# A hybrid mLSTM and gated-delta encoder block: modulation rows in a tile of their own, asked for three quanta ahead of pinned sums

## The chip, the cores and the metric

The kernel runs on one core of a Trainium2 chip. The core's engines run side by side, each through its own list of instructions in order: TensorE (PE; its weight loads are PEld), VectorE (DVE), ScalarE (ACT), GpSimd (POOL) and SyncE (SP). Here SP does nothing but ask for transfers (DMA) from the chip's memory into the core's on-chip memory. An instruction that waits for a semaphore holds up all that stands behind it on its engine. The metric is the device time of one execution in microseconds (us); lower is better.

## The reference, cut to what matters

One encoder block on a sequence of 256 tokens with 2048 channels, everything in float32:

```python
mod = silu(c) @ ada_w + ada_b                      # (1, 6 * 2048)
shift_m, scale_m, gate_m, shift_f, scale_f, gate_f = jnp.split(mod, 6, axis=-1)
h = rms_norm(x, norm_mix_w) * (1 + scale_m) + shift_m
(a_q, a_k, a_v, a_o, a_i, a_f, b_qkv, b_z, b_beta, b_a, merge) = split(h @ w_in)
y_a = (sigmoid(a_o) * rms_norm(mlstm(...))) @ w_branch_a      # 4 heads, both directions
y_b = (rms_norm(gated_delta(...)) * silu(b_z)) @ w_branch_b   # 16 heads, both directions
g_a, g_b = split(sigmoid(merge))
x = x + gate_m * ((g_a * y_a + g_b * y_b) @ w_out)
hf = rms_norm(x, norm_ffn_w) * (1 + scale_f) + shift_f
gt, up = split(hf @ w_gate_up)
x = x + gate_f * ((silu(gt) * up) @ w_down)
return rms_norm(x, norm_final_w)
```

The change touches how the last four of the six modulation vectors come to be: gate_m, shift_f, scale_f and gate_f, 2048 numbers each, each a dot product of silu(c) with a column of ada_w.

## The kernel before

**Weights.** Almost all time goes into products of 256 tokens with weight matrices. A weight tile is 1 MB (128 partitions x 2048 numbers, 8 KB in a partition). SP asks for it (line 181 in `fjob`, line 213 in `tjob`) into a ring of three buffers with the tag "raw". Float32 is emulated by a high and a low part: for each half of the tile ACT rounds the high part `wh` (lines 185, 216), DVE subtracts to get the low part `wl` (lines 187, 218), and PE makes three products of each block, `wh` with the high part of the activations, `wh` with their low part, and `wl` with the high part (lines 190 to 192 and 237 to 239). A buffer of the ring is free again once DVE has made `wl` of its second half. A half tile is one step of a job, and the change calls it a quantum. `fjob` puts features on the partitions and makes gated-delta and mLSTM heads (tiles named raw_b, raw_a), `tjob` puts tokens there (raw_z, raw_ma, raw_mb, raw_o, raw_yb, raw_ya, and raw_gt, raw_up, raw_d in the FFN).

**Stages.** The modulation's first two parts are folded into the first product (to about 137 us of the profile). The gates and the first heads follow until 310. Then 16 gated-delta heads go in four groups of four. Each group runs two pairs of heads (`gdn_phase2`, `gdn_blocks`) and then the inversion for the next group (`invert`); the groups' pairs lie at 310 to 440, 495 to 605, 690 to 810 and 870 to 965. These recurrences are chains of small operations on PE, DVE and ACT. Between their steps the code calls `next(pieces)` or `fill()`, which runs one step of a weight job, so that PE has dense work while a chain waits. The mLSTM and the projection `y_b` follow to 1100, then `y_a` and the output projection to 1270, then the FFN: gate and up to 1744, down to 1976.

**The modulation rows.** Parts 2 to 5 are laid out so that a row block is again 128 x 2048 numbers, 1 MB: 16 blocks to a part, 64 in all, named ada2_0 to ada5_15. `add()` (line 114) multiplies a block by silu(c) and sums over the row, one DVE instruction of 2048 columns, whose result is 128 of the part's numbers. `ada_parts` is a generator that hands out these blocks in turn, and `pump()`, called once for every two half tiles, takes a step of it on every `every[0]`-th call. `held` keeps steps back in the first pieces of a pair, and `owed` remembers them. `room` says where the blocks go. In the gated-delta, mLSTM and y_b stages and in the FFN it is the same ring "raw" that the weights stream through, with at most one block asked for at a time; at y_a and the output projection it is a pool of its own, "sr", with three buffers. In the ring's first use a block's sum is added either when the next block is due or when two more weight tiles have been asked for (`raw_tile`).

**What sets the order.** The instructions are written in this order and then moved by a list scheduler; `order(...)` (`keep_in_program_order`) pins an instruction to its place in the program. The sums are pinned only where `room[0][3] > 1`, at y_a and the output projection; elsewhere the scheduler places them. On SP rows and weights stand in one queue.

Of the kernel before, what the change touches and what calls it, by code (L numbers as in the profile page):

```python
# [9 lines left out]
F32 = mybir.dt.float32  # L10
# [5 lines left out]
P = 128  # L16
# [36 lines left out]
def hybrid_block(ctx: ExitStack, tc: tile.TileContext, xr, nfr, crow, pk_d, cst_d, ada2, ada4, win0, winb, wint, wba, wbb, wo, wgu, wd, out, dbg=None):  # L53
# [6 lines left out]
    cp = pool(ctx, "cp")  # L60
    st = pool(ctx, "st")
    acc_ps = pool(ctx, "acc_ps", 4, space=PSUM)
    g_ps = pool(ctx, "g_ps", 4, space=PSUM)
# [42 lines left out]

    room = [(st, "raw", 3, 0)]
    asked, since = [], [0]

    def add():  # L110

        part, b, raw = asked.pop(0)
        c = part * KB + b
        order(V.scalar_tensor_tensor(raw, raw, 1.0, row_c[:, :D], ALU.mult, ALU.mult, accum_out=mod[:, c : c + 1]), room[0][3] > 1)  # L114
        if b == KB - 1:
            c = slice(part * KB, part * KB + KB)
            V.tensor_tensor(mod[:, c], mod[:, c], pk[:, PK_ADAB + c.start : PK_ADAB + c.stop], ALU.add)

    def ada_parts(*parts):

        todo = [(part, b) for part in parts for b in range(KB)]
        while todo or asked:
            pl, tag, bufs, depth = room[0]
            if not depth and asked:
                add()
            while todo and len(asked) < max(depth, 1):
                part, b = todo.pop(0)  # L130
                raw = pl.tile([P, D], F32, tag=tag, bufs=bufs, name=f"ada{part}_{b}")
                nc.sync.dma_start(raw, ada4[part - 2, b])
                asked.append((part, b, raw))
                since[0] = 0
            if depth:
                add()
            yield True

    def raw_tile(shape, name):

        since[0] += 1
        if since[0] > 2 and asked and room[0][0] is st:
            add()
        return st.tile(shape, F32, tag="raw", bufs=3, name=name)
# [10 lines left out]

    background = []
    count, every = [0], [0]
    owed, held = [0], [False]

    def sums(n=1):  # L160

        while n and background:
            if next(background[0], None):
                n -= 1
            else:
                background.pop(0)

    def pump():
        count[0] += 1
        if every[0] and count[0] % every[0] == 0:  # L170
            owed[0] += 1
        if owed[0] and not held[0]:
            owed[0] -= 1
            sums()

    def fjob(name, src, done):

        ps = acc_ps.tile([P, 512], F32, tag="acc", name=f"acc_{name}")
        o = ps[:, :T]
        raw = raw_tile([P, KB, P], f"raw_{name}")  # L180
        nc.sync.dma_start(raw, src)
        for k0 in range(0, KB, 8):
            wh = st.tile([P, 8, P], F32R, tag="wh", bufs=3, name=f"wh_{name}_{k0}")
            wl = st.tile([P, 8, P], F32R, tag="wl", bufs=3, name=f"wl_{name}_{k0}")
            S.activation(wh, raw[:, k0 : k0 + 8], AF.Copy)  # L185
            settle()
            V.tensor_tensor(wl, raw[:, k0 : k0 + 8], wh.bitcast(F32), ALU.subtract)  # L187
            for k in range(8):
                kk = k0 + k
                PE.matmul(o, wh[:, k], woven(hh[:, kk]), start=kk == 0, stop=False)  # L190
                PE.matmul(o, wh[:, k], woven(hl[:, kk]), start=False, stop=False)  # L191
                PE.matmul(o, wl[:, k], woven(hh[:, kk]), start=False, stop=kk == KB - 1)  # L192
            if k0:
                pump()
                done(o.rearrange("p (c h) -> p h c", h=2))
            yield True
# [5 lines left out]
    def tjob(name, chunks, xh, xl, done, early=0, by_token=None, steps=1, parts=((0, slice(0, 512)), (1, slice(0, 512)))):  # L202
# [28 lines left out]
        for n, (u, k0) in enumerate(todo):  # L231
            wh, wl = made.pop(0) if made else halves(u, k0)
            for k in range(2):
                kk = 4 * u + k0 + k
                for t in range(2):
                    c = slice(t * P, (t + 1) * P)
                    order(PE.matmul(ps[t], xh[:, kk, c], woven(wh[:, k]), start=kk == 0, stop=False), early and steps > 1)  # L237
                    PE.matmul(ps[t], xl[:, kk, c], woven(wh[:, k]), start=False, stop=False)  # L238
                    PE.matmul(ps[t], xh[:, kk, c], woven(wl[:, k]), start=False, stop=kk == last)  # L239
            if k0:  # L240
                pump()
                if u == len(chunks) - 1:
                    done(ps)
# [767 lines left out]
    for pair in ((0, 1), (2, 3)):  # L1011
# [5 lines left out]
        for n, _ in enumerate(steps(*(heads1[h] for h in pair))):  # L1017
            fill(3 + n)
    background.append(ada_parts(2, 3, 4))

# [8 lines left out]
    for g in range(4):  # L1029
# [6 lines left out]
        if g == 3:  # L1036
# [4 lines left out]
            for c in first2:  # L1041
                next(c)
        every[0] = (4, 2, 2, 2)[g]
        for p in range(2):
# [17 lines left out]
        if g < 3:  # L1062
            fills.insert(0, z_job(g + 1))
            every[0] = owed[0] = 0
            if asked:
                add()
            invert(g + 1)
# [58 lines left out]
    every[0] = owed[0] = 0  # L1126
    if asked:
        add()
    cores = steps(*first2)
# [23 lines left out]
    drive(cores, 3)  # L1153
    every[0] = 2
    drive(steps(mlstm(2), mlstm(3)), 3)
    every[0] = 1
    fill(1000)
# [29 lines left out]

    every[0] = 2
    for g in range(4):
# [134 lines left out]
    if dbg is not None and "x1" in dbg:  # L1324
        G.dma_start(dbg["x1"], x1)
    room[0] = (st, "raw", 3, 1)
    background.append(ada_parts(5))
    sw.close()
# [71 lines left out]
    next(gt0)  # L1400
    every[0] = 4

# [168 lines left out]
```

## Time and profile before

| | us |
|---|---|
| runs of the kernel: median of 3 | 1991.46 |
| lowest, highest | 1991.42, 1999.04 |
| profiled execution | 1994.34 |
| its span, first to last instruction | 1992.4 |
| TensorE clock granted, mean over the span | 0.991 of full |

The profiled execution is 2.9 us above the median, and 1.9 us of it lie outside its span. The span is what the views divide: busy time of an engine is the time in which one of its instructions runs; a wait is idle time of an engine with the instruction that ended it; the chain of waits goes back from an instruction to what released it. All times in the views count from the start of the span. In the names, wh_a is the high part of a tile raw_a, acc_a the product that uses it, and ada<-ada a block of modulation rows.

### The profile page before, as it was taken

To read this page: it belongs to the slowest core of one execution; us is meant where nothing else is said; L and a number is where in the kernel's file an instruction comes from. 1 tells how busy PE (TensorE), PEld (TensorE's weight loads), DVE (VectorE), ACT (ScalarE), POOL (GpSimd) and SP (SyncE) were. 2 spreads that over 40 slices of the span, in tenths; PEclk is the share of its full clock that TensorE was granted. 3 is DMA by queue.
4 is the path that set the end of the run, shared out by engine and by line. 5 is a ranking of instruction groups with operands and counts; after the bars stand their busy time and mean duration, and the time that the engine had idled before them with its cause. 6 is when DMAs were issued, how large, how long until landed. Compare 5 with 4: busy or idle time off the path is not lost.

```text
span 1992.4 us, 27101 instructions
## 1 busy us (share of the span) xinstructions
PE 1937.3 (97%) x10418; PEld 1708.8 (86%) x10418; DVE 1407.0 (71%) x2067; ACT 1032.8 (52%) x1557; POOL 116.4 (6%) x211
## 2 busy tenths in 40 slices
PE   8999999999999999999999999999999999999998
PEld 6878889998898899889787888888888888888886
DVE  6778887887878798867476878765666665555554
ACT  3137647765666576555444544554444444444444
POOL 0001210111001101010100000200000000000000
PEclk9999999999999999999999999999999999999999
DMA  9987676655667666587786888566676675565653
GB/s 399 420 338 232 190 250 231 222 182 199 232 191 231 222 235 210 197 278 265 255 303 230 351 300 325 176 239 247 235 268 237 234 269 194 200 212 201 210 194 145
DMA packets 78962, 485.64 MB, mean 244 GB/s; under 512 B 10585, under 2 KB 15969, under 8 KB 24433
## 3 DMA queue, kind: packets, MB, share of 16 engines
q1 hardware_dynamic: 63216, 450.69, 62.6%
q0 software_dynamic: 8160, 17.88, 4.0%
q10 hardware_dynamic: 7458, 15.36, 2.0%
q8 instruction: 81, 1.33, 0.3%
q14 instruction: 47, 0.39, 0.1%
HBM read 467.07 MB, written 16.82 MB: 243 GB/s over the span
## 4 chain that ended last, share of the span: by engine, by line
PE 76%; DVE 10%; DMA 8%; ACT 2%; issue 2%; POOL 0%; ACTq 0%; SPq 0%; DVEq 0%; POOLq 0%
PE acc_gt L238 4%; PE acc_gt L237 4%; PE acc_gt L239 4%; PE acc_up L238 4%; PE acc_up L237 4%; PE acc_up L239 4%; PE acc_d L237 4%; PE acc_d L238 4%; PE acc_d L239 4%; DMA ra<-ada 3%; PE acc_o L239 2%; PE acc_o L237 2%; PE acc_o L238 2%; DMA ada<-ada 2%; PE acc_b L190 2%
## 5 line engine op out<-in xcount | busy, mean ns | idle before, releaser
L218 DVE TENSOR_TENSOR wl_d<-raw_d,wh_d 128x1024 fp32r<-128x1024 f32 x88 | 107.7, 1225 | 105.9 <-ACT wh_d L216 105.9
L218 DVE TENSOR_TENSOR wl_up<-raw_up,wh_up 128x1024 fp32r<-128x1024 f32 x88 | 107.7, 1225 | 100.3 <-ACT wh_up L216 100.3
L218 DVE TENSOR_TENSOR wl_gt<-raw_gt,wh_gt 128x1024 fp32r<-128x1024 f32 x88 | 108.2, 1229 | 79.6 <-ACT wh_gt L216 79.5
L190 PE MATMUL acc_b<-hh,wh_b 128*128 128x256 f32 x576 | 163.4, 284 | 0.4 <-ACT wh_b L185 0.4
L192 PE MATMUL acc_b<-hh,wl_b 128*128 128x256 f32 x576 | 160.2, 278 | 1.0 <-DVE wl_b L187 0.9
L191 PE MATMUL acc_b<-hl,wh_b 128*128 128x256 f32 x576 | 159.6, 277 | 0.0
L216 ACT ACTIVATE wh_d<-raw_d 128x1024 fp32r<-128x1024 f32 x88 | 93.0, 1057 | 126.3 <-PE acc_d L238 117.6
L114 DVE SCALAR_TENSOR_TENSOR ada<-ada,crow 128x2048 f32<-128x2048 f32 x64 | 146.4, 2288 | 14.8 <-DMA ada<-ada 14.7
L216 ACT ACTIVATE wh_gt<-raw_gt 128x1024 fp32r<-128x1024 f32 x88 | 92.9, 1056 | 118.6 <-PE acc_gt L238 71.0
L216 ACT ACTIVATE wh_up<-raw_up 128x1024 fp32r<-128x1024 f32 x88 | 92.8, 1055 | 108.1 <-PE acc_up L238 77.1
L237 PE MATMUL acc_gt<-wh_gt,hfh 128*128 128x512 f32 x352 | 135.5, 385 | 0.6 <-ACT hfh L1358 0.6
L238 PE MATMUL acc_gt<-wh_gt,hfl 128*128 128x512 f32 x352 | 135.2, 384 | 0.0
L239 PE MATMUL acc_gt<-wl_gt,hfh 128*128 128x512 f32 x352 | 134.0, 381 | 0.0
L237 PE MATMUL acc_up<-wh_up,hfh 128*128 128x512 f32 x352 | 133.4, 379 | 0.0
L238 PE MATMUL acc_up<-wh_up,hfl 128*128 128x512 f32 x352 | 133.4, 379 | 0.0
L239 PE MATMUL acc_up<-wl_up,hfh 128*128 128x512 f32 x352 | 133.4, 379 | 0.0
L237 PE MATMUL acc_d<-wh_d,ffh 128*128 128x512 f32 x344 | 130.5, 379 | 0.0
L238 PE MATMUL acc_d<-wh_d,ffl 128*128 128x512 f32 x344 | 130.5, 379 | 0.0
L239 PE MATMUL acc_d<-wl_d,ffh 128*128 128x512 f32 x344 | 130.4, 379 | 0.0
L564 PE MATMUL first<-x,raw 128*128 128x256 f32 x512 | 114.5, 382 | 7.6 <-ACT x L558 7.6
L564 PEld LDWEIGHTS first<-x,raw 128*128 128x128 f32 x512 | 96.0, 190 | 26.1 <-ACT x L558 13.6
L192 PEld LDWEIGHTS acc_b<-hh,wl_b 128*128 128x128 f32 x576 | 111.7, 194 | 1.7 <-DVE wl_b L187 1.7
(383 smaller groups left out, 5283.6 us busy)
## 6 DMA issues: line engine op xcount, KB each, us to landing
ada<-ada SPq DMA_DIRECT2D x64, 1024.0 KB, 5.0
raw_gt<-wgu SPq DMA_DIRECT2D x44, 1024.0 KB, 5.0
raw_up<-wgu SPq DMA_DIRECT2D x44, 1024.0 KB, 4.9
raw_d<-wd SPq DMA_DIRECT2D x44, 1024.0 KB, 4.9
raw_b<-winb SPq DMA_DIRECT2D x36, 1024.0 KB, 5.2
ra<-ada SPq DMA_DIRECT2D x32, 1025.0 KB, 15.7
raw<-win SPq DMA_DIRECT2D x16, 1024.0 KB, 14.5
raw_z<-wint SPq DMA_DIRECT2D x16, 1024.0 KB, 5.3
```

What stands on the lines that cost most here:

```text
L114: order(V.scalar_tensor_tensor(raw, raw, 1.0, row_c[:, :D], ALU.mult, ALU.mult, accum_out=mod[:, c : c + 1]), room[0][3] > 1)
L190: PE.matmul(o, wh[:, k], woven(hh[:, kk]), start=kk == 0, stop=False)
L191: PE.matmul(o, wh[:, k], woven(hl[:, kk]), start=False, stop=False)
L192: PE.matmul(o, wl[:, k], woven(hh[:, kk]), start=False, stop=kk == KB - 1)
L216: order(S.activation(wh, raws[u][:, k0 : k0 + 2], AF.Copy), early)
L218: order(V.tensor_tensor(wl, raws[u][:, k0 : k0 + 2], wh.bitcast(F32), ALU.subtract), early)
L237: order(PE.matmul(ps[t], xh[:, kk, c], woven(wh[:, k]), start=kk == 0, stop=False), early and steps > 1)
L238: PE.matmul(ps[t], xl[:, kk, c], woven(wh[:, k]), start=False, stop=False)
L239: PE.matmul(ps[t], xh[:, kk, c], woven(wl[:, k]), start=False, stop=kk == last)
L564: PE.matmul(first[o], raw[:, o], x[:, b], start=b == 0 and o % 2 == 0, stop=b == KB - 1 and o % 2 == 1)
```

## The change

A pool "rows" with one tile of 8 KB in a partition is added, and the blocks of rows use it in the stages in which they used the ring (`room[0] = (rows_p, "ada", 1, 1)`); the pool of three at y_a and the output projection stays. Asking and adding are two functions: `ask()` issues the transfer, `add()` the sum, and both are pinned to their place in the program. `pump()` is called for each half tile, so twice as often as before. It asks for the next block when none is asked for. It adds a block only when more than two quanta have gone by since it was asked for (`age`), when a sum is owed, and when `held` is off. A sum is owed on every `every[0]`-th call, at most one at a time: every call in the gated-delta and y_b stages, where the age alone then limits them to one in four quanta, every fourth at y_a, and every eighth in the FFN. The adds that `raw_tile` made and those at the end of a group are gone. The on-chip scratch for POOL's transfer descriptors is set to 8192 bytes in a partition.

```diff
@@ -59,6 +59,7 @@
 
     cp = pool(ctx, "cp")
     st = pool(ctx, "st")
+    rows_p = pool(ctx, "rows")
     acc_ps = pool(ctx, "acc_ps", 4, space=PSUM)
     g_ps = pool(ctx, "g_ps", 4, space=PSUM)
     sa, sx, sf = ExitStack(), ExitStack(), ExitStack()
@@ -104,43 +105,32 @@
         order(S.activation(row_c[:, g * 512 : (g + 1) * 512], pc_, AF.Silu))
 
 
-    room = [(st, "raw", 3, 0)]
-    asked, since = [], [0]
+    room = [(rows_p, "ada", 1, 1)]
+    asked, unasked, age = [], [], [0]
+
+    def ask():
+
+        pl, tag, bufs, _ = room[0]
+        part, b = unasked.pop(0)
+        raw = pl.tile([P, D], F32, tag=tag, bufs=bufs, name=f"ada{part}_{b}")
+        order(nc.sync.dma_start(raw, ada4[part - 2, b]))
+        asked.append((part, b, raw))
+        age[0] = 0
 
     def add():
 
         part, b, raw = asked.pop(0)
         c = part * KB + b
-        order(V.scalar_tensor_tensor(raw, raw, 1.0, row_c[:, :D], ALU.mult, ALU.mult, accum_out=mod[:, c : c + 1]), room[0][3] > 1)
+        order(V.scalar_tensor_tensor(raw, raw, 1.0, row_c[:, :D], ALU.mult, ALU.mult, accum_out=mod[:, c : c + 1]))
         if b == KB - 1:
             c = slice(part * KB, part * KB + KB)
             V.tensor_tensor(mod[:, c], mod[:, c], pk[:, PK_ADAB + c.start : PK_ADAB + c.stop], ALU.add)
 
     def ada_parts(*parts):
-
-
-
-
-        todo = [(part, b) for part in parts for b in range(KB)]
-        while todo or asked:
-            pl, tag, bufs, depth = room[0]
-            if not depth and asked:
-                add()
-            while todo and len(asked) < max(depth, 1):
-                part, b = todo.pop(0)
-                raw = pl.tile([P, D], F32, tag=tag, bufs=bufs, name=f"ada{part}_{b}")
-                nc.sync.dma_start(raw, ada4[part - 2, b])
-                asked.append((part, b, raw))
-                since[0] = 0
-            if depth:
-                add()
-            yield True
+        unasked.extend((part, b) for part in parts for b in range(KB))
 
     def raw_tile(shape, name):
 
-        since[0] += 1
-        if since[0] > 2 and asked and room[0][0] is st:
-            add()
         return st.tile(shape, F32, tag="raw", bufs=3, name=name)
 
 
@@ -153,25 +143,32 @@
             behind.remove(f)
             f()
 
-    background = []
     count, every = [0], [0]
     owed, held = [0], [False]
 
     def sums(n=1):
 
-        while n and background:
-            if next(background[0], None):
-                n -= 1
-            else:
-                background.pop(0)
+        while n and (unasked or asked):
+            while unasked and len(asked) < room[0][3]:
+                ask()
+            add()
+            n -= 1
 
     def pump():
         count[0] += 1
+        age[0] += 1
         if every[0] and count[0] % every[0] == 0:
-            owed[0] += 1
-        if owed[0] and not held[0]:
-            owed[0] -= 1
-            sums()
+            owed[0] = 1
+        if room[0][3] > 1:
+            if owed[0]:
+                owed[0] = 0
+                sums()
+        elif asked:
+            if owed[0] and age[0] > 2 and not held[0]:
+                owed[0] = 0
+                add()
+        elif unasked and every[0]:
+            ask()
 
     def fjob(name, src, done):
 
@@ -190,8 +187,8 @@
                 PE.matmul(o, wh[:, k], woven(hh[:, kk]), start=kk == 0, stop=False)
                 PE.matmul(o, wh[:, k], woven(hl[:, kk]), start=False, stop=False)
                 PE.matmul(o, wl[:, k], woven(hh[:, kk]), start=False, stop=kk == KB - 1)
+            pump()
             if k0:
-                pump()
                 done(o.rearrange("p (c h) -> p h c", h=2))
             yield True
 
@@ -237,8 +234,8 @@
                     order(PE.matmul(ps[t], xh[:, kk, c], woven(wh[:, k]), start=kk == 0, stop=False), early and steps > 1)
                     PE.matmul(ps[t], xl[:, kk, c], woven(wh[:, k]), start=False, stop=False)
                     PE.matmul(ps[t], xh[:, kk, c], woven(wl[:, k]), start=False, stop=kk == last)
+            pump()
             if k0:
-                pump()
                 if u == len(chunks) - 1:
                     done(ps)
             yield True
@@ -1016,7 +1013,7 @@
                 fill(2)
         for n, _ in enumerate(steps(*(heads1[h] for h in pair))):
             fill(3 + n)
-    background.append(ada_parts(2, 3, 4))
+    ada_parts(2, 3, 4)
 
     def invert(g):
         gen = gdn_invert(g)
@@ -1040,7 +1037,7 @@
             first2 = [mlstm(h) for h in range(2)]
             for c in first2:
                 next(c)
-        every[0] = (4, 2, 2, 2)[g]
+        every[0] = 1
         for p in range(2):
             pieces = stream(4 * g + 2 * p + 4)
             for n in range(1, 10):
@@ -1062,8 +1059,6 @@
         if g < 3:
             fills.insert(0, z_job(g + 1))
             every[0] = owed[0] = 0
-            if asked:
-                add()
             invert(g + 1)
     settle()
     sx.close()
@@ -1124,8 +1119,6 @@
 
     o4s = [o_load(g) for g in range(2)]
     every[0] = owed[0] = 0
-    if asked:
-        add()
     cores = steps(*first2)
     fill(1)
     next(cores)
@@ -1151,9 +1144,8 @@
     o_split(3, o4s[3])
     fill(2)
     drive(cores, 3)
-    every[0] = 2
+    every[0] = 1
     drive(steps(mlstm(2), mlstm(3)), 3)
-    every[0] = 1
     fill(1000)
     mgh, mgl = big(bigC, F32R, "mgh"), big(bigC, F32R, "mgl")
     sm_.close()
@@ -1185,7 +1177,7 @@
             PE.matmul(pr, onesr, woven(dg[:, i]), start=i == 0, stop=i == 1)
         S.activation(woven(dst[:, g * 512 : (g + 1) * 512]), pr.rearrange("p (c h) -> p c h", h=2), AF.Copy)
 
-    every[0] = 2
+    every[0] = 4
     for g in range(4):
         for i, _ in enumerate(y_a(g)):
             if g and i == 3:
@@ -1323,8 +1315,8 @@
                 )
     if dbg is not None and "x1" in dbg:
         G.dma_start(dbg["x1"], x1)
-    room[0] = (st, "raw", 3, 1)
-    background.append(ada_parts(5))
+    room[0] = (rows_p, "ada", 1, 1)
+    ada_parts(5)
     sw.close()
     sr_.close()
     sc.close()
@@ -1398,7 +1390,7 @@
             for t in range(2):
                 normed(b // 4 + 1, t, slice(0, 512), G)
     next(gt0)
-    every[0] = 4
+    every[0] = 8
 
     for j in range(FB // 4):
         run(gate(j) if j else gt0)
@@ -1558,7 +1550,7 @@
     from concourse.bass_utils import run_bass_kernel_spmd as _run
 
     arrays = _arrays(**{k: np.asarray(v) for k, v in inputs.items()})
-    nc = _bacc.Bacc("TRN2", target_bir_lowering=False, num_devices=1)
+    nc = _bacc.Bacc("TRN2", target_bir_lowering=False, num_devices=1, dynamic_dma_scratch_size=8192)
     args = [
         nc.dram_tensor(name, a.shape, mybir.dt.from_np(a.dtype), kind="ExternalInput").ap() for name, a in arrays.items()
     ]
```

Three places in the order of the instructions follow. A row is the line of code, the operation, what it writes<-what it reads, and the size; ada2_5 is the sixth block of part 2, raw_b9_0 the first tile of head 9's job, and the number at the end of a name is the program's count of tiles. The changed kernel's line numbers are its own: 116 is the transfer of a block and 124 its sum, 178 and 210 the weight tiles' transfers, 215 `wl`, 1089 the merge of y_b.

The first is SP in the second gated-delta group, at the tiles of head 9. Before:

```order
L181 DMA raw_b9_0_4606<-winb 128x2048
L132 DMA ada2_5_4666<-ada4 128x2048
L181 DMA raw_b9_1_4704<-winb 128x2048
L181 DMA raw_b9_2_4822<-winb 128x2048
L132 DMA ada2_6_4887<-ada4 128x2048
L181 DMA raw_a1_2_4961<-winb 128x2048
L132 DMA ada2_7_5038<-ada4 128x2048
L181 DMA raw_a1_3_5044<-winb 128x2048
```

and now:

```order
L178 DMA raw_b9_0_4618<-winb 128x2048
L116 DMA ada2_7_4597<-ada4 128x2048
L178 DMA raw_b9_1_4713<-winb 128x2048
L178 DMA raw_b9_2_4834<-winb 128x2048
L116 DMA ada2_8_4772<-ada4 128x2048
L178 DMA raw_a1_2_4971<-winb 128x2048
L178 DMA raw_a1_3_5053<-winb 128x2048
L178 DMA raw_b10_0_5142<-winb 128x2048
L116 DMA ada2_9_5001<-ada4 128x2048
```

The transfers of blocks have moved: before there is one every one to two weight tiles, now one every two to three, and they no longer stand for a turn of the weights' ring. By the same tile of head 9 the changed kernel is two blocks further.

The second is DVE where y_a begins. wl_ya0_0_2 is the second half of y_a's first tile, mg the merge of y_b's last product, wl_ya0_1_0 the first half of y_a's second tile. Before:

```order
L218 TENSOR_TENSOR wl_ya0_0_2_10287<-raw_ya0_0_10268,wh_ya0_0_2_10286 128x1024
L1094 TENSOR_TENSOR mg_9470<-gtb3_10062,acc_yb3_0_10064 128x512
L1094 TENSOR_TENSOR mg_9470<-gtb3_10062,acc_yb3_1_10065 128x512
L114 TENSOR_SCALAR ada4_0_10302,mod_88<-ada4_0_10302,crow_73 128x2048
L218 TENSOR_TENSOR wl_ya0_1_0_10317<-raw_ya0_1_10314,wh_ya0_1_0_10316 128x1024
```

and now:

```order
L215 TENSOR_TENSOR wl_ya0_0_2_10290<-raw_ya0_0_10264,wh_ya0_0_2_10289 128x1024
L1089 TENSOR_TENSOR mg_9464<-gtb3_10059,acc_yb3_0_10061 128x512
L1089 TENSOR_TENSOR mg_9464<-gtb3_10059,acc_yb3_1_10062 128x512
L124 TENSOR_SCALAR ada3_13_10247,mod_91<-ada3_13_10247,crow_76 128x2048
L124 TENSOR_SCALAR ada3_14_10282,mod_91<-ada3_14_10282,crow_76 128x2048
L124 TENSOR_SCALAR ada3_15_10284,mod_91<-ada3_15_10284,crow_76 128x2048
L215 TENSOR_TENSOR wl_ya0_1_0_10317<-raw_ya0_1_10314,wh_ya0_1_0_10316 128x1024
```

Where one sum stood between mg and wl_ya0_1_0, three stand now, blocks 13 to 15 of part 3.

The third is SP at the same place. Before:

```order
L213 DMA raw_ya0_1_10314<-wba 128x2048
L213 DMA raw_ya0_2_10352<-wba 128x2048
L132 DMA ada4_0_10302<-ada4 128x2048
L132 DMA ada4_1_10304<-ada4 128x2048
L132 DMA ada4_2_10306<-ada4 128x2048
```

and now:

```order
L210 DMA raw_ya0_1_10314<-wba 128x2048
L116 DMA ada3_13_10247<-ada4 128x2048
L116 DMA ada3_14_10282<-ada4 128x2048
L116 DMA ada3_15_10284<-ada4 128x2048
L116 DMA ada4_0_10286<-ada4 128x2048
L210 DMA raw_ya0_2_10352<-wba 128x2048
```

Four blocks stand ahead of y_a's third tile, raw_ya0_2, where before they stood behind it.

## The prediction

> **What bounds the kernel now.** I read the page first, its busy times and the chain that ended last.
>
> ```profile
> span 1992.4 us, 27101 instructions
> PE 1937.3 (97%) x10418; PEld 1708.8 (86%) x10418; DVE 1407.0 (71%) x2067; ACT 1032.8 (52%) x1557; POOL 116.4 (6%) x211
> PE 76%; DVE 10%; DMA 8%; ACT 2%; issue 2%; POOL 0%; ACTq 0%; SPq 0%; DVEq 0%; POOLq 0%
> ```
>
> PE is busy for 97% of the span. The change touches neither a matmul nor a byte, so what it can win lies in PE's gaps and in products that run at a lower clock. The next view is the busy time by stretches (seconds column: length; then busy time of PE, PEld, DVE, ACT and POOL, granted clock, DMA share, GB/s). The rows are three stretches of the gated-delta stage, the one in which it runs out, and the FFN's first part.
>
> ```profile
> 495.00:605.00 110.00, 102.18 (x855) 100.14 (x855) 90.58 (x173) 75.26 (x157) 9.89 (x20) 0.97 0.64 211
> 605.00:690.00 85.00, 78.12 (x388) 66.64 (x387) 65.44 (x132) 46.00 (x68) 10.48 (x20) 1.00 0.68 222
> 690.00:810.00 120.00, 114.71 (x899) 110.74 (x897) 102.23 (x207) 87.09 (x178) 9.64 (x19) 0.97 0.66 226
> 870.00:965.00 95.00, 92.14 (x588) 84.91 (x587) 60.99 (x81) 52.04 (x102) 0.53 (x1) 0.98 0.74 273
> 1250.00:1700.00 450.00, 446.86 (x2114) 388.37 (x2114) 282.93 (x285) 211.54 (x246) 10.80 (x6) 1.00 0.65 232
> ```
>
> In the FFN, PE lacks 3 us of 450: there is nothing to win. The gated-delta stretches lack 7.8, 6.9, 5.3 and 2.9 us, and three of them ran below full clock. DVE is the next busiest there, at 82% (90.58 of 110) and 85% (102.23 of 120). The waits of PE in those stretches (who waited for whom: total us, times, longest) name its gaps:
>
> ```profile
> PE vps L612 <- ACT vf L344: 5.3, 2, 4.6
> PE p L798 <- DVE pt L787: 1.3, 1, 1.3
> ...
> PE acc_ma L237 <- ACT wh_ma L216: 2.2, 1, 2.2
> PE acc_ma L239 <- DVE wl_ma L218: 1.6, 2, 1.1
> PE p L764 <- DVE R L733: 1.4, 1, 1.4
> ...
> PE vps L612 <- ACT vf L344: 3.3, 2, 2.7
> PE pa L811 <- DVE UL L747: 1.1, 1, 1.1
> ...
> PE acc_z L237 <- ACT wh_z L216: 2.5, 1, 2.5
> ...
> PE pc L810 <- DVE r L823: 2.3, 1, 2.3
> ```
>
> Together they are 21.0 us; other waits there are 1.0 us or less each. An engine is named, but what is late may be a transfer ahead of that engine's instruction. The chain of waits, followed back from these places, shows it (start, length, what):
>
> ```profile
> 539.88 7.94 DMA raw_a<-winb
> ...
> 547.91 1.06 ACT wh_a L185
> 548.96 0.31 ACT vf L344
> ...
> 565.29 8.19 DMA ada<-ada
> ...
> 573.50 2.30 DVE ada L114 x2
> ...
> 576.20 0.61 DVE pt L787
> ...
> 606.25 7.67 DMA raw_ma<-wint
> ...
> 753.84 9.70 DMA ada<-ada
> ...
> 763.56 2.30 DVE ada L114 x2
> ...
> 943.90 8.07 DMA ada<-ada
> ```
>
> At 548 ACT stands at a weight split whose tile landed late, with the short vf that PE wants behind it. At 573, 763 and 952 DVE stands at a sum whose row landed late, with the recurrence's small operations behind it. The same buffers make both late: rows and weights share the ring of three, and SP, in order, waits for a buffer until a sum has been done:
>
> ```profile
> SPq L213 <- DVE ada L114: 86.4, 28, 8.2
> SPq L181 <- DVE ada L114: 45.8, 11, 7.3
> ```
>
> So weights stood behind sums for 132.2 us in 39 waits. Most was covered; the part that reached PE is in the rows above.
>
> **The change part by part.** *Rows out of the ring.* A gated-delta job that is half done keeps one ring tile, a row keeps another, and weights stream through the third. After the change the weights have the whole ring. I count as removed what the chain ties to the ring: 5.3 (vf behind the late raw_a), 1.3 (pt behind the sum at 573), 2.2 and the smaller half of 1.6, which is 0.5 (wh_ma, wl_ma behind the late raw_ma), two thirds of 3.3 (vf after the sum at 763; one of its two waits I cannot tie), 2.2, and 2.3 (r, and with it pc, behind the sum at 952). The sum is 13.8 us. Bounds: 6.9 if half the rows are late again, 21.0 if every row quoted goes.
>
> *The clock after a gap.* Stretches right behind three of these gaps:
>
> ```profile
> 549.00:556.00 7.00, 6.68 (x33) 6.68 (x34) 3.53 (x15) 4.47 (x9) 0.00 (x0) 0.56 0.29 117
> 774.00:781.00 7.00, 6.63 (x34) 6.63 (x35) 4.12 (x8) 3.99 (x8) 0.00 (x0) 0.58 0.82 300
> 955.00:965.00 10.00, 10.00 (x65) 9.68 (x65) 3.36 (x4) 4.95 (x16) 0.00 (x0) 0.83 0.63 224
> ```
>
> What is lost is the length times the missing clock: 7 x 0.44 = 3.1, two thirds of 7 x 0.42, 1.9 (in the share I took of its gap), and 10 x 0.17 = 1.7. That is 6.7 us that goes with the gaps. With the second stretch whole it is 3.1 + 2.9 + 1.7 = 7.7 us lost behind 4.6 + 2.7 + 2.3 = 9.6 us waited, 0.8 us of clock for each us of a gap. The bounds of the gaps, 6.9 and 21.0, so give 5.5 and 16.8.
>
> The Trainium skill's page "TensorE: Matmul & The Clock Gate", section "What's actually happening", lets the clock fall only after PE has idled through a window of some 3.4 us. By it only the 4.6 us gap would cost clock, the term would be 3.1 and the whole 1980.6. The trace disagrees: 0.58 and 0.83 stand behind gaps of 2.7 and 2.3.
>
> *Sums pinned, one in four quanta.* Their number and size stay:
>
> ```profile
> L114 DVE SCALAR_TENSOR_TENSOR ada<-ada,crow 128x2048 f32<-128x2048 f32 x64 | 146.4, 2288 | 14.8 <-DMA ada<-ada 14.7
> DMA to landing us min/median/max: 4.7/6.3/18.0
> ```
>
> A sum is 2.29 us and a read of 0.08, 2.37. A quantum is half a weight tile, 12 products; from the FFN's row a product of 512 columns is 450 / 2114 = 0.213 us, so a quantum is 2.55 and three are 7.7: the median row (6.3) has landed when its sum comes up, the slowest (18.0) has not. The order shows the second group with two sums fewer, the first with two more. DVE had 82% and 85% there; two sums less are 4.7 us of 120. I set this at zero: the gain is already in the waits.
>
> *The start of y_a.* Here the order shows a new pile. Three sums of modulation part 3 stand in a row on DVE, between the merge of y_b's last product (mg) and the low part of y_a's second tile (wl_ya0_1). Before there was one sum in that place.
>
> ```profile
> 1080.79 1.27 DVE L1094 TENSOR_TENSOR mg<-gtb,acc_yb 128x512 f32<-128x512 f32 x2
> L218 DVE TENSOR_TENSOR wl_ya<-raw_ya,wh_ya 128x1024 fp32r<-128x1024 f32 x32 | 38.6, 1223 | 13.7 <-ACT wh_ya L216 13.6
> ```
>
> mg can only start when PE has ended y_b. DVE then needs 1.27 + 3 x 2.37 + 1.22 = 9.6 us until wl_ya0_1 is there. PE has the two quanta of the first tile, whose parts are made already, and two products of the next, 2 x 2.55 + 0.43 = 5.5 us. So PE stalls for 4.1 us. Before, 1.27 + 2.37 + 1.22 = 4.9 was below 5.5. With 0.5 us of clock for each us of the stall, between none and the 0.8 above, it costs +6.0. Bounds: +2 if the scheduler's cover is one quantum more (4.1 - 2.55 = 1.6), +9 if the four rows that SP now asks for ahead of raw_ya0_2 (4 MB) add one quantum's wait (6.0 + 2.55 = 8.6).
>
> *FFN.* A sum in eight half tiles instead of four whole-tile counts keeps the density. The cover is DVE's idle time ahead of its weight splits, 100.3 us for wl_up alone:
>
> ```profile
> DVE wl_up L218 <- ACT wh_up L216: 100.3, 78, 3.2
> ```
>
> Zero; without that cover 16 x 2.37 = 38 us would lie on PE.
>
> *A smaller descriptor scratch.* The 8 KB for the row tile come out of it. POOL's own transfers are short instructions now:
>
> ```profile
> L666 POOL DMA_DIRECT2D inst_d<-mi x64 | 35.0, 553 | 386.7 <-DVE mi L660 386.6 <-issue 0.2
> ```
>
> I take zero; its price otherwise stands with the rivals.
>
> The sum: -13.8 - 6.7 + 6.0 = -14.5 us. The profiled execution took 1994.34 us, 1.9 more than its span and 2.9 more than the median of the runs, 1991.46. Applied to the median, -14.5 gives **1977.0**. Bounds: with the small gains and the dear pile, -6.9 - 5.5 + 9 = -3.4, 1988.1; with the large ones, -21.0 - 16.8 + 2 = -35.8, 1955.7.
>
> **The rivals.** *Nothing (within 0.5%).* What waited for buffers then waits for DVE. For it: DVE's 82 to 85% in the gated-delta stretches, and that a pinned sum can no longer step back behind the recurrence's small operations, of which each waits up to 2.37 us at it; 10 such meetings would be 23.7 less what PE covers, and six that bare half their length, 7.1, and their clock, 5.7, take back 12.8 of the 14.5: 1989.8. Against it: at 763 the sum's length was not what cost, its row's landing was. A second way to the same time is the scratch: if POOL's transfers wait for room in it once in each of four groups, for some 4 us each, as the gap behind a late weight tile did, +16 gives 1993. The Trainium skill bears on it in "SBUF — State Buffer", section "SBUF size: 192, 224, or 256?", which sets 16 KiB of a partition aside for descriptor scratch, and in "DMA: Bandwidth & Descriptors", section "SWDGE vs HWDGE vs iDMA", which puts software rings there. No run here shows it full.
>
> *Slower.* One mechanism: SP is in order, and there is one row tile. The ask for the next row stands on SP until the last sum is done; where that sum is itself late, all weights asked behind it are late, and the stop falls on PE. Thirty asks lie ahead of y_a. For it: 132.2 us of waits of just this kind today. Against it: an ask is made a quantum after the sum before it, and the sum comes only when its row has had three. One stop costs what the quoted gaps cost, (4.6 + 2.7 + 2.3 + 2.2) / 4 = 2.95, and 0.8 of that in clock: 5.3 us. Three stops use up the gain, five make it slower than 0.5%, and eight of thirty give -14.5 + 42.4 = +27.9, 2019.
>
> *More.* The gaps that I could not tie to the ring (R, UL, z, half of the ma ones) go too, and the pile at y_a hides: 1956, the far bound above, or up to 1966 with part of them.
>
> *It doesn't do what it says.* The rows would still go through the ring; the order shows them in their own tile, so this is left at nothing.
>
> **How the numbers follow.** A measurement of this kernel tells about 0.5%, 10 us, from no change, so faster means below 1981.5 and slower above 2001.4. Forecast, 1966 to 1981.5: 0.49. More, below 1966: 0.14. Nothing, to 2001.4: 0.20, both of its ways and the forecast's own small end. Slower: 0.17. Hence faster 0.63, same 0.20, slower 0.17. The range runs from the far bound, 1956, to 2002: it leaves out some 0.01 below and 0.17 above. The likeliest case's own range is 1966 to 1981.5.
>
> **What would show it.** Right: the waits of SP's weight loads for L114's sums are nearly gone; the vf waits (4.6 and 2.7) and the pc wait are missing from PE's list; clock 1.00 in the second and third group; a PE gap near the start of y_a, about 4 us, for wl_ya. Wrong: PE waits of the old size in the same groups, now for DVE (the nothing case); SP standing at row asks with weights behind them (slower); POOL's issue rows longer than 553 ns (scratch); no gap at y_a.

## The result and the profile after

| | before | changed |
|---|---|---|
| runs, median (us) | 1992.64 (6 runs) | 1974.51 (6 runs, 1972.51 to 1979.65) |
| profiled execution, its span (us) | 1994.34, 1992.4 | 1974.30, 1972.4 |
| TensorE clock granted, mean | 0.991 | 0.994 |

The ratio is 0.9915, with an interval of 0.9891 to 0.9939: the change made the kernel faster, by 18.1 us between the medians. Predicted was 1977.0, which is 14.5 us below the kernel before.

The page of the changed kernel, in the lines that answer to those of before:

```profile
span 1972.4 us, 27079 instructions
PE 1929.4 (98%) x10418; PEld 1703.5 (86%) x10418; DVE 1405.5 (71%) x2067; ACT 1030.0 (52%) x1555; POOL 116.5 (6%) x211
PE 81%; DVE 8%; DMA 6%; ACT 2%; issue 1%; POOL 0%; ACTq 0%; SPq 0%; DVEq 0%; POOLq 0%
```

PE and DVE run as many instructions as before (10418 and 2067); the chain that ended last lies on PE for 81% instead of 76%, and less of it on DVE and on transfers. Where the time went, the stretches of both kernels show, cut at the same places of the program: the first group, the second with its inversion, the third, the fourth with the first mLSTM heads, y_b, and y_a. The columns are as in the prediction. Before:

```profile
310.00:485.00 175.00, 173.24 (x1192) 161.79 (x1191) 144.77 (x288) 117.58 (x216) 20.33 (x40) 1.00 0.64 211
485.00:690.00 205.00, 189.14 (x1316) 175.23 (x1315) 160.25 (x309) 127.82 (x236) 20.37 (x40) 0.98 0.64 210
690.00:870.00 180.00, 172.37 (x1226) 162.51 (x1225) 150.42 (x298) 117.88 (x218) 22.98 (x43) 0.97 0.67 223
870.00:998.00 128.00, 125.14 (x723) 109.39 (x722) 79.36 (x112) 70.23 (x131) 9.24 (x15) 0.97 0.73 265
998.00:1103.00 105.00, 104.64 (x479) 86.61 (x478) 75.66 (x104) 49.29 (x69) 1.16 (x3) 0.98 0.74 272
1103.00:1191.00 88.00, 88.00 (x421) 77.10 (x421) 71.57 (x75) 40.61 (x43) 0.00 (x0) 1.00 0.86 328
```

After:

```profile
310.00:485.00 175.00, 171.95 (x1175) 159.97 (x1174) 150.18 (x298) 119.98 (x222) 20.42 (x40) 1.00 0.68 220
485.00:670.00 185.00, 179.34 (x1281) 168.78 (x1280) 151.90 (x298) 119.62 (x224) 20.36 (x40) 0.99 0.66 217
670.00:850.00 180.00, 175.91 (x1273) 165.87 (x1272) 150.20 (x300) 122.52 (x227) 22.96 (x43) 0.99 0.66 218
850.00:972.00 122.00, 121.95 (x727) 107.21 (x726) 76.76 (x110) 70.04 (x132) 7.69 (x13) 1.00 0.74 263
972.00:1077.00 105.00, 104.96 (x481) 87.03 (x480) 76.56 (x104) 50.86 (x70) 2.71 (x5) 0.98 0.75 275
1077.00:1171.00 94.00, 90.19 (x421) 77.98 (x420) 76.35 (x81) 40.51 (x42) 0.00 (x0) 0.98 0.85 324
```

Length minus PE's busy time is PE's idle time. From the second group to the end of y_b it was 15.86 + 7.63 + 2.86 + 0.36 = 26.7 us and is now 5.66 + 4.09 + 0.05 + 0.04 = 9.8: 16.9 us of gaps are gone. The first group gave 1.3 back (1.8 idle, now 3.1). Length times the missing clock was 4.1 + 5.4 + 3.8 + 2.1 = 15.4 and is 1.9 + 1.8 + 0 + 2.1 = 5.8, 9.6 less; the clock has two digits, so this is good to some 3 us. In windows of half a microsecond the same sums are 13.7 and 5.1, so 8.5 less. Gaps of 16.9 less the 1.3, with 8.5 to 9.6 of clock, give 24.1 to 25.2, and y_b begins 25.5 us earlier (998.1, now 972.6). y_a, in contrast, lost. Its first products with the high part, from first to last start, before and after:

```profile
L237 PE MATMUL acc_ya<-wh_ya,hah x128: 379/379/463, 1103.7 to 1190.3; 128*128 128x512 f32 x128
```

```profile
L234 PE MATMUL acc_ya<-wh_ya,hah x128: 379/379/631, 1077.7 to 1170.4; 128*128 128x512 f32 x128
```

y_a begins 26.0 us earlier and takes 92.7 us instead of 86.6 (first to last start). So -26.0 + 6.1 = -19.9, which is the difference of the spans, 20.0; behind y_a nothing changed. What PE still waits for, by the view of waits, from the second group to the end of y_b and then at the start of y_a:

```profile
PE acc_z L234 <- ACT wh_z L213: 2.5, 1, 2.5
PE vps L609 <- ACT vf L341: 2.4, 2, 1.4
PE p L770 <- DVE pt L762: 1.0, 1, 1.0
...
PE acc_ya L236 <- DVE wl_ya L215: 3.8, 2, 2.2
```

The vf wait of 4.6 us, the one of 2.7, and the pc wait of 2.3 are missing. The wait for wh_z was there before, with the same 2.5 us; in both kernels ACT makes that wh_z right behind an obt of its own, not behind a late tile. No weight load on SP waits for a sum any more; in their place SP stands at the asks for rows:

```profile
SPq L116 <- DVE ada L124: 193.9, 55, 8.7
```

### The profile page after: what moved, and what is told of

Its sections match the earlier page's. It is cut to its first block, busy times and chain, and to the rows that moved or that the text cites. A ratio compares the mean times of both kernels' runs of the same rounds, so it can differ in the third digit from the quotient of the medians.

```text
span 1972.4 us, 27079 instructions
## 1 busy us (share of the span) xinstructions
PE 1929.4 (98%) x10418; PEld 1703.5 (86%) x10418; DVE 1405.5 (71%) x2067; ACT 1030.0 (52%) x1555; POOL 116.5 (6%) x211
## 4 chain that ended last, share of the span: by engine, by line
PE 81%; DVE 8%; DMA 6%; ACT 2%; issue 1%; POOL 0%; ACTq 0%; SPq 0%; DVEq 0%; POOLq 0%
PE acc_gt L234 4%; PE acc_gt L235 4%; PE acc_gt L236 4%; PE acc_up L236 4%; PE acc_up L235 4%; PE acc_up L234 4%; PE acc_d L236 4%; PE acc_d L235 4%; PE acc_d L234 4%; DMA ra<-ada 3%; PE acc_b L187 2%; PE acc_b L188 2%; PE acc_b L189 2%; PE acc_o L236 2%; PE acc_o L234 2%; PE acc_o L235 2%
## 6 DMA issues: line engine op xcount, KB each, us to landing
ra<-ada SPq DMA_DIRECT2D x32, 1025.0 KB, 15.8
raw<-win SPq DMA_DIRECT2D x16, 1024.0 KB, 14.5
```

## The experiments

Each kernel was timed in five rounds beside the kernel before on the same chip; the ratios are to that. Edits are to the kernel named. Starts of stages are from one profile each: of the changed kernel and of the one without the pile there are two, in which y_b begins at 972.6 and 976.2, and at 973.8 and 972.1, so differences of 2 to 4 us between single profiles tell nothing.

**The tile alone** (to the kernel before; descriptor scratch at 8192, sums and asks unpinned):

```diff
-    room = [(st, "raw", 3, 0)]
+    room = [(rows_p, "ada", 1, 0)]
...
-        if since[0] > 2 and asked and room[0][0] is st:
+        if since[0] > 2 and asked and room[0][0] is rows_p:
...
-    room[0] = (st, "raw", 3, 1)
+    room[0] = (rows_p, "ada", 1, 1)
```

> The kernel before, with a row tile of its own (and the smaller descriptor scratch that makes room for it); asking, adding and pinning stay as they were. Theory ring: what was gained is that weights get the third ring buffer, so this alone gives the 20.5 us of the first two terms and no pile at y_a: about 1972 us, the 4.6, 2.7 and 2.3 us waits (vf twice, pc) gone, no weight load on SP waiting for a sum. Rival rules: the gain comes from the lead of three quanta and from one pinned sum in four, and the tile alone leaves the late rows in front of the recurrence: 1987 to 1993 us with waits behind sums of the old size.

2016.92 us, 1.0128 (1.0108 to 1.0149): slower by 24 us, which neither theory had. The rows of the sums, in the stage before the first group and in its pairs, show why:

```profile
L115 DVE SCALAR_TENSOR_TENSOR ada<-ada,crow x13: 2262/2280/2293, 140.7 to 304.5; 128x2048 f32<-128x2048 f32 x13
...
L115 DVE SCALAR_TENSOR_TENSOR ada<-ada,crow x11: 2283/2285/2293, 313.7 to 440.0; 128x2048 f32<-128x2048 f32 x11
```

24 sums have begun by 440 us, where in the kernel before it was four. With a buffer of their own, transfer and sum depend on nothing around them, and the scheduler moved them forward, into a stage in which DVE was the next limit:

```profile
150.00:310.00 160.00, 152.43 (x736) 130.99 (x735) 151.70 (x281) 98.23 (x148) 25.07 (x47) 1.00 0.84 286
310.00:440.00 130.00, 121.84 (x914) 116.63 (x913) 112.79 (x212) 88.47 (x180) 14.20 (x28) 0.96 0.72 249
```

DVE is busy for 151.70 us of 160 there, 136.72 before, and PE's busy time fell from 158.50 and 129.80 to 152.43 and 121.84, 14.0 us of new gaps; the clock of 0.96, 1.00 before, is some 5 us more. The shared ring had also been what held the sums in their place; the pins, below, test that.

**The new rules in the old ring** (to the changed kernel, its pool "rows" dropped):

```diff
-    room = [(rows_p, "ada", 1, 1)]
+    room = [(st, "raw", 3, 1)]
...
-    room[0] = (rows_p, "ada", 1, 1)
+    room[0] = (st, "raw", 3, 1)
```

> The changed kernel with the blocks of rows back in the ring of three (before y_a and in the FFN), the new rules of asking, adding and pinning kept. Theory ring: a row now holds a ring buffer for some four quanta, so weights stream through one buffer again, longer than before the change: 1990 to 2010 us, SP weight loads waiting for sums 130 us or more in total. Rival rules: most of the gain stays, 1975 to 1982 us.

2052.63 us, 1.0309 (1.0286 to 1.0331). Weight loads wait for sums again, and PE for weights that landed late:

```profile
SPq L209 <- DVE ada L123: 77.0, 28, 10.8
...
SPq L177 <- DVE ada L123: 37.1, 8, 8.4
```

```profile
PE acc_b L186 <- ACT wh_b L181: 14.1, 6, 4.0
PE acc_z L233 <- ACT wh_z L212: 9.9, 4, 4.3
PE acc_ya L233 <- ACT wh_ya L212: 7.9, 2, 5.8
```

The total of 114.1 us is below the 130 expected and the mean wait no longer than before (3.2 us, before 3.4); the longest is (10.8 us, before 8.2), and PE now waits 31.9 us for the high parts in these three rows. The time is 43 us beyond the expected range: the rules alone make it worse by more than expected, and they need the tile.

**A fourth buffer for the shared ring** (to the kernel before; scratch at 8192):

```diff
-    room = [(st, "raw", 3, 0)]
+    room = [(st, "raw", 4, 0)]
...
-        return st.tile(shape, F32, tag="raw", bufs=3, name=name)
+        return st.tile(shape, F32, tag="raw", bufs=4, name=name)
```

(the ring's three other uses likewise)

> The kernel before, with the freed 8 KB spent on a fourth buffer of the shared ring instead of a row tile; sums unpinned and at the old cadence. Theory buffers: the weights lacked a buffer, whoever holds it, so this gains about what the change gained before y_a: 1970 to 1976 us. Rival order: where sums stand on DVE carries most of the change, so a fourth buffer alone gives little or lets the scheduler move sums forward as it did with the tile alone: 1986 to 2015 us.

1979.61 us, 0.9922 (0.9892 to 0.9951): 3.6 us above the first theory's range and 6.4 below the rival's.

```profile
L237 PE MATMUL acc_yb<-wh_yb,obh x128: 379/379/780, 979.0 to 1087.3; 128*128 128x512 f32 x128
```

y_b begins at 979.0, where it was 998.1 before and 972.6 with the change; y_b then takes 3 to 4 us longer than in either, so that y_a, which has no pile and takes 86.6 us, begins at 1088.0 (1103.7 before, 1077.7 with the change). The same 8 KB, given to the ring without any new rule, bring 19.1 of the 25.5 us that the change brings up to y_b, and 15.7 of 26.0 up to y_a. In the medians, on one chip, it is 15.8 us, and 21.7 with the change, pile and all (1973.64, below). So most of what was lost was a buffer, whoever holds it. The waits of weight loads for sums were not the loss in themselves: with four buffers there are 166.9 us of them in 36, more than the 132.2 before. DVE still stands in front of late rows with four buffers, with the change never; what this costs was not taken apart from the rest.

```profile
DVE ada L114 <- DMA ada<-ada: 27.2, 19, 4.0
```

**Tile and pins, the old cadence** (to the kernel of the tile alone):

```diff
-        order(V.scalar_tensor_tensor(..., accum_out=mod[:, c : c + 1]), room[0][3] > 1)
+        order(V.scalar_tensor_tensor(..., accum_out=mod[:, c : c + 1]))
...
-                nc.sync.dma_start(raw, ada4[part - 2, b])
+                order(nc.sync.dma_start(raw, ada4[part - 2, b]))
```

> The kernel before with a row tile of its own and with asks and sums pinned; the old cadence (a step on every second or fourth tile, sum and next ask together) and the count per whole tile stay. Theory ring and pins: these two are the whole change, and the pile at y_a isn't there: 1968 to 1975 us. Rival rules: the gap of a quantum between sum and next ask and the limit of one in four are needed: 1985 us or more, with sums in front of the recurrence.

1979.94 us, 0.9928 (0.9905 to 0.9950): 4.9 us above the first theory's range and 5.1 below the rival's. The pins turn the tile alone from +1.3% to -0.7%, and nothing else differs between the two kernels. y_b begins at 983.0, 10.4 us later than with the change (8.5 by the start of y_a), and y_a takes 87.3 us.

**The sums unpinned** (to the changed kernel; the asks stay pinned):

```diff
-        order(V.scalar_tensor_tensor(..., accum_out=mod[:, c : c + 1]))
+        order(V.scalar_tensor_tensor(..., accum_out=mod[:, c : c + 1]), room[0][3] > 1)
```

> The changed kernel with the sums in the row tile not pinned (their asks stay pinned, and so do the sums at y_a). The first run of the tile alone was slower by 24 us because transfers and sums, held by nothing any more, moved up into the stage before the first group. Theory pins: the pins carry the change as much as the tile; here the asks still hold the sums back, so only their place between two asks is free, and the waits behind sums come back in part: 1976 to 1990 us. Rival: pinning the asks is enough: 1970 to 1976 us.

1987.42 us, 0.9967 (0.9950 to 0.9984). As expected of the pins: the sums step forward to where their rows haven't landed, and DVE waits in front of them.

```profile
DVE ada L124 <- DMA ada<-ada: 16.9, 12, 3.1
```

**One sum in two quanta** (to the changed kernel):

```diff
-            if owed[0] and age[0] > 2 and not held[0]:
+            if owed[0] and age[0] > 0 and not held[0]:
```

> The changed kernel with a sum already one quantum after its ask instead of three, so one in two quanta. Theory lead: a quantum is 2.55 us and a row needs 4.7 at least, so DVE stands in front of the recurrence again, for 2 us and more at each of some thirty sums; DVE is 82 to 85% busy there: 1985 to 2005 us, idle DVE ahead of sums 15 us or more (none in the changed kernel). Rival: the lead does not matter once SP asks from a tile of its own: 1972 to 1978 us.

2010.74 us, 1.0079 (1.0054 to 1.0103), a little beyond the range. Idle DVE ahead of sums is back, and 12 sums lie in the first group's pairs, where the change has 6. The row for DVE:

```profile
DVE ada L124 <- DMA ada<-ada: 26.4, 17, 4.6
```

The edit shortens the lead and packs the sums at once, so it doesn't tell which of the two costs.

**One in five before y_a, one in two there** (to the kernel without the pile, below):

```diff
-            if owed[0] and age[0] > 2 and not held[0]:
+            if owed[0] and age[0] > 3 and not held[0]:
...
-    every[0] = 3
+    every[0] = 2
```

> The kernel of e3 with at most one sum in five quanta before y_a, and one in two at y_a, where five sums more now stand. Theory DVE: fewer sums in the groups leave the recurrence's small operations freer, and y_a bears one in two only just (per two quanta 2 x 1.22 + 2.37 = 4.8 us of DVE against 5.1 of PE, before the merges): the groups 1 to 4 us shorter, y_a 0 to 8 longer: 1965 to 1975 us. Rival: one in four is already free of cost and y_a too: 1967 to 1970 us, both stages as in e3.

1993.07 us, 0.9997 (0.9977 to 1.0017): both expectations missed. y_a takes 99.3 us, with DVE busy for 88.05 of 100 and PE waiting for the merges, so it doesn't bear one in two. But the groups were slower too: y_b begins at 983.2, 9.4 and 11.1 us later than in the two profiles of the kernel it was made from. PE's waits for vf are 6.8 us in eight, where they were 2.7 in three:

```profile
PE vps L609 <- ACT vf L341: 6.8, 8, 1.4
```

It isn't the number of sums: the pairs of the first group hold six of them in both kernels, and PE's vf waits there are 2.2 us, where they were 0.3. They stand elsewhere among the recurrence's operations; what each place costs was not traced. One in four is better than one in two and one in five, but not because of the density of sums alone.

**No pile at y_a** (to the changed kernel):

```diff
-    if asked:
-        add()
     room[0] = (pool(sr_, "sr"), "sr", 3, 3)
...
-    every[0] = 4
+    count[0] = owed[0] = 0
+    every[0] = 3
```

> The changed kernel with the three sums at the start of y_a spread: no sum at the switch of pools, the count starts anew there, and one sum in three quanta (ten sums in y_a as in the change). Theory pile: the waits of acc_ya for wl_ya (3.8 us) go and the clock behind them stays at 1.00: y_a shorter by 5 to 6 us, about 1968.5 us. Rival: the sums come due later and the lost time returns at the output projection or at the FFN's start: 1974.5 us, with a new wait there.

1968.74 us, 0.9889 (0.9869 to 0.9909), as expected. PE waits for no wl_ya any more, y_a takes 87.3 us, and nothing came back later: the FFN begins 5.8 us earlier than with the change. In the profile of the second run, below, y_a takes 86.6 us, the FFN begins 6.5 us earlier, PE has no gap in the stage, and its clock is full:

```profile
1077.00:1164.00 87.00, 87.00 (x416) 76.37 (x415) 75.31 (x80) 40.37 (x42) 0.00 (x0) 1.00 0.89 344
```

It was run again with the changed kernel on one chip:

> The changed kernel again, beside e3 on one chip: 0.9915 of the kernel before, as at first, within 0.002.

> The kernel of e3 again, beside the change on one chip: 5.4 us of y_a's stage shorter than the change, so 0.9888 of the kernel before, and below the change by 4 to 7 us. Rival: the difference of the two first runs came from different chips: equal within 2 us.

1973.64 us, 0.9896 (0.9875 to 0.9917), for the change, and 1969.59 us, 0.9872 (0.9848 to 0.9896), without the pile. The medians differ by 4.1 us; the intervals overlap, so it is the stage that tells the two apart, in each of two profiles (PE's wait for wl_ya is 3.8 us in both of the change and absent from both without the pile). This is the best version found.

**The scratch alone** (to the kernel before): `dynamic_dma_scratch_size=8192`, nothing else.

> The kernel before with the descriptor scratch of 8192 bytes and nothing else. The prediction priced it at zero: 1992.6 us within 3, POOL's issue rows at their 553 ns. Rival: POOL's transfers wait for room: up to 16 us slower, in the inversions, with longer issue rows on POOL.

1994.84 us, 1.0014 (0.9999 to 1.0029). POOL's issues took what they took:

```profile
L666 POOL DMA_DIRECT2D inst_d<-mi x64 | 35.0, 553 | 389.2 <-DVE mi L660 368.3 <-DVE wl_z L218 20.7
```

**Rows asked for by POOL** (to the kernel without the pile):

```diff
-        order(nc.sync.dma_start(raw, ada4[part - 2, b]))
+        order(G.dma_start(raw, ada4[part - 2, b]))
```

> The kernel of e3 (no pile) with the rows asked for by POOL instead of SP, so that no weight load stands behind an ask that waits for the last sum (55 such waits, 193.9 us in the changed kernel). Theory covered: with three buffers the weights are asked for early enough, and these stops cost PE nothing: 1966 to 1972 us, or some us more where POOL's own transfers come late. Rival stops: they cost a part of what is left in the groups: 1955 to 1964 us.

1976.75 us, 0.9913 (0.9890 to 0.9935), against 0.9889 and 0.9872 for its parent on other chips: no gain, and some loss is likely, though the intervals overlap. The SP stops are gone, and the time didn't fall. POOL now asks late, since its own transfers wait in the same line, and DVE stands in front of three rows:

```profile
DVE ada L124 <- DMA ada<-ada: 12.9, 3, 6.7
```

## Why the prediction was right, and where it was not

**The shared ring's gaps: right, nearly in size.** Forecast -13.8, measured -16.9 from the second group on and +1.3 in the first, so -15.6. In the rows quoted, 21.0 us of waits became 6.0, so 15.0 went. It wasn't quite the choice made: R (1.4) and UL (1.1), which I had left out because the chain didn't tie them to the ring, went, while of the vf waits, 8.6 us, 2.4 stayed, for which I had left 1.1. The 2.5 us for wh_z, also left out, stayed.

**The clock behind them: right in kind, wrong as a price.** Forecast -6.7; measured 8.5 to 9.6 less in one pair of profiles, and only some 5 less by the second profile of the change. All the runs say it better: the span times what the mean granted clock lacks of 1 is 19.4 us on average in the 51 runs of the kernel before beside the experiments and 11.5 in the 12 of the change, 7.9 less, although the pile at y_a cost 1.7 anew. But the time isn't lost in proportion to a gap, as the forecast's 0.8 us for each us of gap has it. In windows of half a microsecond each drop of the clock in the groups, in y_b and at y_a is to half, for some 3.4 us, which costs 1.7 us, or for twice as long, which costs 3.4. At y_a one gap of PE has such a drop behind it and the next has none:

```profile
1086.49 0.93 PE L236 MATMUL acc_ya<-wl_ya,hah 128*128 128x512 f32 x2 [2.15 <-DVE wl_ya L215]
1082.00:1090.00 8.00, 5.85 (x20) 4.52 (x19) 8.00 (x10) 2.55 (x3) 0.00 (x0) 0.80 0.96 323
...
1097.00:1104.00 7.00, 5.34 (x25) 4.38 (x24) 4.70 (x5) 3.55 (x4) 0.00 (x0) 1.00 0.92 345
1104.00:1120.00 16.00, 16.00 (x79) 13.97 (x78) 15.00 (x16) 7.69 (x9) 0.00 (x0) 1.00 0.78 292
```

The second gap, 1.66 us, lies in the third of these rows. In the two profiles of the change the gap of 1.4 us for vf near 581 has a drop behind it in one and none in the other, and the drop behind wh_z lasts 3.4 us in one and 7 in the other. And some drops have no gap ahead of them. One of these, not among the three of the forecast, is in the kernel before:

```profile
975.00:985.00 10.00, 10.00 (x38) 7.63 (x38) 4.19 (x10) 3.81 (x5) 2.65 (x5) 0.83 1.02 380
...
973.26 2.57 PE pden L965 x24
```

PE was busy ahead of it, with 24 products of one column each. Behind the same 24 the first profile of the change has no drop and the second has one; behind the next such run, in y_b, one of the two profiles without the pile has a drop and the other none. So part of the clock's gain in any one pair of profiles is luck, and the sum's closeness with it.

The rule of the Trainium skill, "TensorE: Matmul & The Clock Gate", section "What's actually happening", by which only an idle window of some 3.4 us costs clock, doesn't hold at y_a, where the clock fell behind a gap of 2.15 us.

**Sums pinned, one in four: the step that failed.** I set this part at zero and gave the whole gain to the tile. The time came out, the attribution didn't: the sum was right for tile and rules together, and its terms were wrong for the tile. The tile alone costs 24 us, the rules in the ring 60, both together bring 18. A buffer for the weights is worth 15.8 us by the ring of four; to get it from a tile of their own, the rows must be pinned, since nothing else holds them (tile and pins: -0.7%), and the lead and spacing, which no run took apart, bring some 10 us more up to y_b. I read the ring as a limit only and missed that it was also what ordered the sums.

**The pile at y_a: right in place, its size partly luck.** Forecast +6.0 (4.1 and half as much for the clock would be 6.15), measured +6.1. The trace of DVE shows the pile as it was worked out (mg, three sums, wl_ya), and behind it another stop:

```profile
1077.39 1.28 DVE L1089 TENSOR_TENSOR mg<-gtb,acc_yb 128x512 f32<-128x512 f32 x2
1078.58 2.28 DVE L124 SCALAR_TENSOR_TENSOR ada<-ada,crow 128x2048 f32<-128x2048 f32 x1
...
1080.80 2.29 DVE L124 SCALAR_TENSOR_TENSOR ada<-ada,crow 128x2048 f32<-128x2048 f32 x1
...
1083.01 2.28 DVE L124 SCALAR_TENSOR_TENSOR ada<-ada,crow 128x2048 f32<-128x2048 f32 x1
...
1085.22 1.22 DVE L215 TENSOR_TENSOR wl_ya<-raw_ya,wh_ya 128x1024 fp32r<-128x1024 f32 x1
...
1098.41 1.29 DVE L1167 TENSOR_TENSOR dg<-cst,mods 128x512 fp32r<-128x512 f32 x2 [3.09 <-PE row L1177]
```

From mg's start to wl_ya's end it is 9.05 us, for the 9.6 of the forecast. But PE had some 7 us of work meanwhile, not the 5.5, so it waited 2.15 us there, not 4.1, with one drop of the clock behind it. The rest, 1.66 us, came at 1099, ahead of a wl_ya that stood behind DVE's wait of 3.09 us for PE's row of a modulation part; the prediction has no such wait, and together the two pieces make 3.8. Spreading the sums took both away.

**FFN and scratch at nothing: right.** From y_a's end on both kernels take the same time, and the scratch alone changes no more than 0.3%.

**The rivals.** *Slower* fell in its price, not in its place: SP does stop at the asks, 55 times for 193.9 us, but with the ring of three free for weights PE's longest wait left in the groups is the old one for wh_z, and taking the stops away brought no gain (POOL's late rows blur that test, so a fraction of a per cent stays open). *Nothing* did not occur, but its mechanism, sums that keep DVE from the recurrence, may be real: one sum in two quanta is slower than the kernel before, though there DVE also stands in front of rows that haven't landed (26.4 us). *More* was half right: R and UL went, z stayed, and the pile did not hide. Of the signs named, one failed: the clock in the second and third group is 0.99, a drop in each, not 1.00.

## What to carry to other kernels

A ring that two streams share does two things: it limits both, and it keeps one in step with the other. Whoever gives one stream a buffer of its own must put an order in place of the ring's, or a scheduler will move the freed work to where it hurts; here the pins alone were the difference between +24 us and -15. After such a move, look at the seams between stages, where the old hand-over and the new count may both let work through at once: a stage that began with three sums in a row gave back 6.1 of the 26.0 us won ahead of it.

## What the runs showed of the hardware

A queue that stands at asks for 193.9 us in total showed no cost on PE in the changed kernel, where the weights behind it have three buffers to be early in; in the kernel before, where one was left to stream through, a late load cost PE up to 4.6 us at once. How long weight loads stand behind sums tells little by itself: 166.9 us with a ring of four, in a kernel 15.8 us faster than the one with 132.2.

The granted clock of PE fell in steps, not in proportion to a gap. In the groups, in y_b and at y_a each drop is to half for some 3.4 us, 1.7 us lost, or for twice that. Drops came behind gaps of some 1 to 4.6 us, but not behind each gap of such a length (none behind one of 1.66 us at y_a and one of 2.25 us in the kernel before, at 615), and behind 2.6 us of one-column products with no gap at all. The same place of the same program had a drop in one profile and none in another, so the clock lost in a single profile is uncertain by a few of these steps.
